# GpSimd issues the stores and loads of the attention's squares, and the first value projection goes by x tile in three column groups

## The chip, the core and the metric

The kernel runs on one core of one Trainium2 chip. The core has five engines with queues of their own, each executed in order: PE (TensorE, matrix products), DVE (VectorE), ACT (ScalarE), POOL (GpSimd) and SP (SyncE, which here only issues DMAs). DMAs are issued from SP's queue and from POOL's. The metric is the device time of one execution in microseconds (us); lower is better.

## The reference

A trunk of two layers works on 1024 tokens of width 1024. Layer 0 mixes tokens by chunked gated linear attention (GLA) with 4 heads, layer 1 by sparse attention with 16 heads in which an indexer lets each query see 256 keys. Both mixers are gated, projected back, added to the residual and normalized; a small gated term with a matrix `p` follows. Cut to what matters here:

```python
def gla_mixer(x, ...):                 # layer 0
    h = x @ w_in                       # q, k, v, z, a
    v = h[..., 2*qk : 2*qk + D_INNER]  # the value projection: 4 heads of 512 columns
    ...
def dsa_mixer(x, ...):                 # layer 1, blocks of 128 queries
    score = einsum(relu(qi @ ki), wi) ; idx = top_k(score, 256)
    logits = q @ k_sel * ATTN_SCALE    # 16 heads share one k and one v
    probs = softmax(logits)
    o = probs @ v_sel
    return (o * silu(z)) @ w_out

x = layer_norm(ALPHA * x + mixer(x))
x = x + (p[i] @ ple_w[i]) * sigmoid(x @ ple_gate_w[i])
```

All is float32. The kernel does each large product as three products of split parts: high times high, high times low, low times high.

## The kernel before

**Stages.** The sequence is cut into two halves of 512 tokens. Layer 0 runs half 0 and half 1, then layer 1 runs half 0 and half 1. In the times of the profile, layer 0's first half starts at 0, its second at about 525 us; layer 1's attention of the first half runs from about 1075 to 1390 us, of the second from about 1480 to 1860 us. "First half" and "second half" below mean these.

**Who sets the order.** The program is written by one planner (`Flow`): generators yield after each small group of PE products, and between groups a heap of due pieces is worked off. The due times are in the planner's own modelled time and decide only in which order instructions enter each engine's queue. On the chip each engine takes its queue in order and waits on semaphores.

**Layer 0's first block.** `v_phase` computes the values of one head: four PSUM banks (128 tokens each) are filled from eight tiles of x, which arrive in turn and are split into high and low parts. A weight pair (`whi`, `wlo`, taken by `W.take`) covers two x tiles: column group c of four holds x tiles 2c and 2c + 1 (kk = 0 and 1). Every step is three products (L58): xh times hi, xh times lo, xl times hi. The usual order is bank by bank with both x tiles in each; in group 0 of head 0, in either half, all four banks take x tile 0 first and then x tile 1.

**Layer 1's attention of one head.** `attend` makes the steps of one head. `A` computes the logits on PE and their minima on DVE (L1592), ACT takes the exponentials (L1599) into the tile `sq`, and DVE turns `sq` in blocks of 32 by 32 in place (L1605). The rest of the transposition goes through DRAM: `store` (L1618) writes each quarter of the partitions of `sq` to a DRAM tile `sqd`, four DMAs of 256 KB for each part, and `load` (L1628) reads that part back as `PT` in one DMA of 1 MB. The first half has one part per head, the second half two (`nb = half + 1`), so 4 stores and 1 load, or 8 stores and 2 loads. Then ACT copies each key group's high part to `ph` (L1645), DVE leaves the low part in `PT` (L1643), and PE multiplies both by the values (L58, `o<-ph,vT` and `o<-PT,vT`). There is one `sq`, `PT` has two buffers per part in the first half and one in the second. The logits of head h + 1 and its stores lie in the slot in which head h is multiplied by the values.

**The inverse sums.** For most heads DVE turns the row sums' inverses and POOL stores them to `row` in four tiny DMAs (L1664); for the others SP stores them (L1676). SP loads `row` to all partitions as `inv` (L1684), and DVE multiplies the gate by it (L1706).

**The queues.** SP issues the weights of layer 1 (L174, ready-made high and low parts from DRAM, 512 KB each, two tiles `whi` and `wlo` per block), the stores and loads of the squares, `inv` and the final stores. POOL issues, beside `row`: `xk` (L1279) and `ys` (L1260), which in layer 0's second half and the attention of the first half turn the residual for layer 1, and `y` (L1264), eight loads at the start of the attention of each half. POOL also clears `sq` (L1825) and does a few small operations of the norms. On each of the two queues the program uses eight semaphores in turn for its DMAs.

Of the kernel before, what the change touches and what calls it, by code (L numbers as in the profile page):

```python
# [10 lines left out]
F32 = mybir.dt.float32  # L11
# [36 lines left out]
class Flow:  # L48
# [6 lines left out]
    def mm(self, out, lhsT, rhs, start, stop):  # L55
        n = out.shape[-1] if len(out.shape) == 2 else math.prod(out.shape[1:])
        slow = lhsT.dtype != BF16 and (lhsT.dtype == F32 or n < 256)
        self.pe.matmul(out, lhsT, rhs, start=start, stop=stop)  # L58
        self.now += n * (4 if slow else 1) / 2400.0
# [218 lines left out]
def trunk_kernel(ctx, tc, x_tok, x_T, p_T, pos, freq, g_q, g_k, g_v, g_z, g_a, g_a2, g_ba, g_gn, g_o,  # L278
                 d_q, d_k, d_v, d_z, d_qi, d_ki, d_o, ln_gb, ple_c, gate_c, out):
    nc = tc.nc  # L280
    act, dve, pool = nc.scalar, nc.vector, nc.gpsimd
# [125 lines left out]
    def pbank():  # L407
        return psum[0].tile([128, 512], F32, tag="pb", name="pb", bufs=psum[1])
# [4 lines left out]
    def split(hi, lo, src, done=None):  # L413

        def second():
            lo_part(lo, src, hi)
            if done:
                done()
        chain((0, lambda: act.activation(hi, src, AF.Copy)), (0.9, second))  # L419
# [77 lines left out]
    def t2k(tag, dt=F32, bufs=8):  # L497
        return lp.tile([128, 512], dt, tag=tag, name=tag, bufs=bufs)
# [85 lines left out]
    def v_phase(u, X):  # L584
        h = u["h"]
        banks = [pbank(), pbank()] + [pp.tile([128, 512], F32, tag="U", name="U", bufs=2) for _ in range(2)]
        for c in range(4):
            hi, lo = W.take(("v", h, c))
            order = [(t, kk) for t in range(4) for kk in range(2)]
            if c == h == 0:  # L590
                order.sort(key=lambda x: x[1])
            for t, kk in order:
                ts = slice(t * 128, t * 128 + 128)
                xh, xl = X[2 * c + kk]
                ws = slice(kk * 512, kk * 512 + 512)
                first, last = c == 0 and kk == 0, c == 3 and kk == 1
                mm(banks[t], xh[:, ts], hi[:, ws], first, False)
                mm(banks[t], xh[:, ts], lo[:, ws], False, False)
                mm(banks[t], xl[:, ts], hi[:, ws], False, last)
                yield  # L600
                if last:
                    vh, vl = t2k("v", F32R), t2k("v", F32R)

                    def done(vh=vh, vl=vl, t=t):
                        u["v"][t] = vh, vl
                    split(vh, vl, banks[t], done)
# [731 lines left out]
    for half in range(NH):  # L1338
# [27 lines left out]
        for h, u in enumerate(units):  # L1366
# [4 lines left out]
            if h == 0:  # L1371
                fl.run(v_phase(u, X))
                for _ in feeder:
                    pass
                ready = a_phase(X, u.pop("wah"))
                if half == 0:
                    bg.set(rope_tables(), 1.7)

                def first_z():
                    zp = z_phase(u, X)  # L1380
                    for i, _ in enumerate(zp):
                        if i == 6:
                            fl.need(lambda: ready)
                            g_phase(u, ready[0])
                        yield
                fl.run(first_z(), qk_phase(u, X))
                g_load(1)
                load_y()
                if half == 0:
                    bg.finish()  # L1390
                    bg3.set(W.split_ahead(later, lp, xp), 2.06)
            else:
                fl.need(lambda: "w2" in u)
                g_phase(u, ready[0])
                fl.run(v_phase(u, X), qk_phase(u, X))
# [159 lines left out]
    def attend(st, h, half, ap, sq):  # L1555
# [11 lines left out]
        def get(*keys):  # L1567
            fl.req(*(k in st for k in keys))
            return [st[k] for k in keys]
# [40 lines left out]
        def store(i):  # L1610

            def f():
                get(*(("D", h, t) for t in range(4)))
                fl.req(st["x"] == nb * h + i)
                dt = st["dram", h, i] = dp.tile([4, 32, 4, HT], F32, tag=f"sq{i}", name="sqd", bufs=2)
                sq4 = sq.rearrange("p (b i c) -> p i b c", b=4, i=nb)
                for a in range(4):
                    nc.sync.dma_start(dt[:, :, a].rearrange("b p c -> p b c"), sq4[32 * a:32 * a + 32, i])  # L1618
                st["x"] += 1
            return f  # L1620

        def load(i):

            def f():
                dt, _ = get(("dram", h, i), ("dram", h, nb - 1))
                fl.req(st["pv"] >= (h * G - (0 if i else G - 4) if half else (h - 1) * G))
                PT = ap.tile([128, 4, HT], F32R, tag=f"PT{i}", name="PT", bufs=2 - half)
                nc.sync.dma_start(PT.bitcast(F32), dt.rearrange("b p a c -> (b p) a c"))  # L1628
                st["PT", h, i] = PT
            return f  # L1630

# [339 lines left out]
```

## Time and profile before

| what | value |
|---|---|
| median of three runs | 1935.55 us (1933.48 to 1938.89) |
| profiled execution: time, span | 1935.94 us, 1934.2 us |
| PE, PEld busy | 1914.7 us, 1590.6 us |
| DVE, ACT, POOL busy | 1495.4, 1002.4, 153.0 us |
| DMA issued by SP (q1), share of 16 engines | 474.55 MB, 72.1% |
| DMA issued by POOL (q0), share of 16 engines | 12.64 MB, 2.0% |

The span goes from the first to the last instruction; the rest of the profiled execution's time lies around it. In a row of a timeline the first number is the start in us from the span's start, the second the duration; a bracket at the end is the idle time of that engine just before and who ended it. In a row of DMA issues stand the number of DMAs, KB of each and the median time from issue to landing. In the view by stretches stand the stretch, its length, then busy time of PE, PEld (weight loads of PE), DVE, ACT and POOL with the number of instructions in brackets, the granted clock of PE, the share of the DMA engines that was busy and GB/s.

### The profile page before, as it was taken

How to read it: one execution, taken by the hardware profiler on the slowest of the kernel's cores; microseconds unless marked ns; L12 is line 12 of the kernel's file. 1: busy time of each engine (PE TensorE's matmuls, PEld its weight loads, DVE VectorE, ACT ScalarE, POOL GpSimd, SP SyncE). 2: the span in 40 equal slices, each digit the busy share in tenths (PEclk: the TensorE clock that was granted, in tenths of full speed). 3: DMA queues.
4: the chain of work that ended last, by engine and by line, in shares of the span. 5: the costliest groups of instructions: out<-in, count | busy, mean ns of one | idle time of the engine just before them, and what ended most of it. 6: DMA issues, size and time to landing. Idle time of an engine off the chain costs nothing.

```text
span 1934.2 us, 26875 instructions
## 1 busy us (share of the span) xinstructions
PE 1914.7 (99%) x8826; PEld 1590.6 (82%) x8826; DVE 1495.4 (77%) x3081; ACT 1002.4 (52%) x1896; POOL 153.0 (8%) x301
## 2 busy tenths in 40 slices
PE   9999999999999999999999999999999999999999
PEld 7888888888888888888888888888888778888887
DVE  5777666696778888878858987778798887777873
ACT  5564636445564646464535676756443443434432
POOL 0000000010010101010101001221001010000000
PEclk9999999999999999999999999999999999999999
DMA  4567766768667767677688588987877898888874
GB/s 156 207 218 230 225 220 215 225 207 274 223 221 262 244 224 247 222 242 228 211 287 302 169 294 288 318 293 283 305 247 283 324 305 302 299 303 289 290 285 142
DMA packets 200764, 488.91 MB, mean 253 GB/s; under 512 B 26504, under 2 KB 42928, under 8 KB 194480
## 3 DMA queue, kind: packets, MB, share of 16 engines
q1 hardware_dynamic: 193200, 474.55, 72.1%
q0 software_dynamic: 7424, 12.64, 2.0%
q8 instruction: 69, 1.13, 0.2%
q14 instruction: 71, 0.58, 0.1%
HBM read 343.18 MB, written 143.92 MB: 252 GB/s over the span
## 4 chain that ended last, share of the span: by engine, by line
PE 88%; DVE 5%; ACT 3%; DMA 2%; issue 1%; SPq 0%; DVEq 0%; ACTq 0%
PE pb L58 67%; PE o L58 8%; PE U L58 6%; PE S L58 5%; DMA PT<-sqd 1%; PE tr L58 1%; DVE sq L1605 1%; DVE PT L1643 0%; DMA wst<-in_g_v 0%; DVE sc L1141 0%; PE xt L62 0%; DVE wlo L191 0%; PE ix L58 0%; SPq L1618 0%; PE S L62 0%
## 5 line engine op out<-in xcount | busy, mean ns | idle before, releaser
L58 PE MATMUL pb<-x,whi 128*128 128x512 f32 x2272 | 704.2, 391 | 0.8 <-DVE x L411 0.7
L58 PEld LDWEIGHTS pb<-x,whi 128*128 128x128 f32 x2272 | 419.5, 188 | 80.0 <-DVE x L411 1.9
L58 PE MATMUL pb<-x,wlo 128*128 128x512 f32 x1136 | 442.6, 390 | 0.0
L58 PE MATMUL pb<-whi,u 128*128 128x512 f32 x1024 | 339.5, 392 | 1.5 <-ACT u L419 0.8
L58 PEld LDWEIGHTS pb<-x,wlo 128*128 128x128 f32 x1136 | 213.2, 188 | 45.8 <-DVE wlo L191 0.4
L58 PEld LDWEIGHTS pb<-whi,u 128*128 128x128 f32 x1024 | 192.2, 188 | 41.3 <-ACT u L419 1.2
L58 PE MATMUL pb<-wlo,u 128*128 128x512 f32 x512 | 199.6, 390 | 0.0
L191 DVE TENSOR_TENSOR wlo<-wst,whi 128x512 fp32r<-128x512 f32 x232 | 154.5, 683 | 35.1 <-ACT whi L189 34.9
L189 ACT ACTIVATE whi<-wst 128x512 fp32r<-128x512 f32 x232 | 136.4, 622 | 73.9 <-DMA wst<-in_g_k 28.8
L1599 ACT ACTIVATE sq<-P,mx 128x128 f32<-128x128 f32 (+7 forms) x128 | 98.8, 772 | 87.6 <-DVE mx L1592 58.0
L58 PE MATMUL S<-kT,q 128*128 128x512 f32 (+2 forms) x576 | 123.6, 343 | 1.7 <-DVE q L411 1.2
L1645 ACT ACTIVATE ph<-PT 128x512 fp32r<-128x512 f32 (+2 forms) x160 | 86.2, 558 | 63.0 <-PE o L58 43.4
L58 PEld LDWEIGHTS S<-kT,q 128*128 128x128 f32 x576 | 100.4, 188 | 20.5 <-DVE mx L1592 2.1
L58 PEld LDWEIGHTS pb<-wlo,u 128*128 128x128 f32 x512 | 96.2, 188 | 18.2
L1643 DVE TENSOR_TENSOR PT<-PT,ph 128x512 fp32r<-128x512 f32 (+2 forms) x160 | 92.6, 592 | 21.4 <-ACT ph L1645 21.2
L1207 ACT ACTIVATE tk<-sc,tki 128x768 f16<-128x768 f32 (+2 forms) x90 | 92.9, 1033 | 25.4 <-DVE tki L1216 21.6
L1605 DVE STREAM_TRANSPOSE sq<-sq 128x128 f32<-128x128 f32 (+7 forms) x128 | 97.7, 768 | 2.0 <-ACT sq L1599 2.0
L237 DVE TENSOR_TENSOR pst<-pst,phi 128x512 fp32r<-128x512 f32 x130 | 88.7, 682 | 7.4 <-ACT phi L233 7.4
L753 ACT ACTIVATE junk<-o 128x512 bf16<-128x512 f32 x32 | 19.1, 597 | 139.7 <-DVE ot L748 116.6
L58 PE MATMUL o<-ph,vT 128*128 128x512 f32 (+2 forms) x320 | 90.8, 365 | 0.0
L58 PE MATMUL pb<-whi,x 128*128 128x512 f32 x256 | 85.3, 392 | 0.0
L58 PE MATMUL U<-whi,x 128*128 128x512 f32 x256 | 84.6, 389 | 0.0
(330 smaller groups left out, 3400.4 us busy)
## 6 DMA issues: line engine op xcount, KB each, us to landing
whi<-whs SPq DMA_DIRECT2D x128, 512.0 KB, 6.1
wlo<-wls SPq DMA_DIRECT2D x128, 512.0 KB, 6.7
sqd<-sq SPq DMA_DIRECT2D x192, 256.0 KB, 4.4
PT<-sqd SPq DMA_DIRECT2D x48, 1024.0 KB, 7.7
whs<-phi SPq DMA_DIRECT2D x130, 256.0 KB, 4.1
wls<-pst SPq DMA_DIRECT2D x130, 256.0 KB, 4.1
wst<-in_g_z SPq DMA_DIRECT2D x32, 512.0 KB, 4.7
wst<-in_g_o SPq DMA_DIRECT2D x32, 512.0 KB, 5.1
```

The lines of the kernel that those rows point to most:

```text
L58: self.pe.matmul(out, lhsT, rhs, start=start, stop=stop)
L189: self.nc.scalar.activation(hi[:, c], st[:, c], AF.Copy, scale=1.0 if gain is None else gain)
L191: self.nc.vector.tensor_sub(lo[:, c], st[:, c], hi[:, c].bitcast(F32))
L237: self.nc.vector.tensor_sub(st, st.bitcast(F32), hi.bitcast(F32))
L753: act.activation(junk, ps, AF.Square, accum_out=u["ss"][:, c:c + 1])
L1207: act.activation(junk()[:, :n], scs[j], AF.Sign, bias=cand[:, j:j + 1].bitcast(F32), accum_out=cnt[:, j:j + 1])
L1599: act.activation(to, rows, AF.Exp, scale=-1.0, bias=mx, accum_out=sm[:, t:t + 1])
L1605: dve.transpose(x, x)
L1643: dve.tensor_sub(lo, lo.bitcast(F32), hi.bitcast(F32))
L1645: chain((0, lambda: act.activation(hi, lo.bitcast(F32), AF.Copy)), (0.8, second))
```

## The change

Two edits. In `v_phase` the condition of the order by x tile was group 0 of head 0 in either half; it is now groups 0, 1 and 2 of head 0 in the first half only. In `attend` the stores of the squares and their loads are issued by `pool` in place of `nc.sync`. Shapes, bytes, tiles and the due times of the planner are unchanged.

```diff
@@ v_phase
             order = [(t, kk) for t in range(4) for kk in range(2)]
-            if c == h == 0:
+            if c < 3 and h == u["half"] == 0:
                 order.sort(key=lambda x: x[1])
@@ attend, store
                 for a in range(4):
-                    nc.sync.dma_start(dt[:, :, a].rearrange("b p c -> p b c"), sq4[32 * a:32 * a + 32, i])
+                    pool.dma_start(dt[:, :, a].rearrange("b p c -> p b c"), sq4[32 * a:32 * a + 32, i])
@@ attend, load
                 PT = ap.tile([128, 4, HT], F32R, tag=f"PT{i}", name="PT", bufs=2 - half)
-                nc.sync.dma_start(PT.bitcast(F32), dt.rearrange("b p a c -> (b p) a c"))
+                pool.dma_start(PT.bitcast(F32), dt.rearrange("b p a c -> (b p) a c"))
```

On PE, group 1 of the first block. `pb_155`, `pb_156`, `U_157` and `U_158` are the four banks, `x_165` and `x_166` the high and low part of x tile 2, `x_190` and `x_191` those of x tile 3. Before:

```order
L58 MATMUL pb_155<-whi_162,x_165 128x512
L58 MATMUL pb_155<-wlo_163,x_165 128x512
L58 MATMUL pb_155<-whi_162,x_166 128x512
L58 MATMUL pb_155<-whi_162,x_190 128x512
L58 MATMUL pb_155<-wlo_163,x_190 128x512
L58 MATMUL pb_155<-whi_162,x_191 128x512
L58 MATMUL pb_156<-whi_162,x_165 128x512
```

And now:

```order
L58 MATMUL pb_155<-whi_162,x_165 128x512
L58 MATMUL pb_155<-wlo_163,x_165 128x512
L58 MATMUL pb_155<-whi_162,x_166 128x512
L58 MATMUL pb_156<-whi_162,x_165 128x512
L58 MATMUL pb_156<-wlo_163,x_165 128x512
L58 MATMUL pb_156<-whi_162,x_166 128x512
L58 MATMUL U_157<-whi_162,x_165 128x512
```

The first product with x tile 3, and with it the second half of the weights' columns, moves from the fourth place to the thirteenth.

On SP, heads 1 and 2 of the second half, before; `whi` and `wlo` are weights, `sqd` the squares in DRAM:

```order
L1618 DMA sqd<-sq 32x4x512 x8
L1628 DMA PT<-sqd 128x2048 x2
L1676 DMA row<-uf 4x128
L174 DMA whi<-whs 128x1024
L174 DMA wlo<-wls 128x1024
L1684 DMA inv<-row 128x512
L1618 DMA sqd<-sq 32x4x512 x8
L174 DMA whi<-whs 128x1024
L174 DMA wlo<-wls 128x1024
L1628 DMA PT<-sqd 128x2048
```

On POOL, the start of the second half and heads 0 to 2, now (before, the eight `y` stood together and behind them only the `row` stores):

```order
L1264 DMA y<-ys_12411 128x512
L1618 DMA sqd<-sq 32x4x512 x8
L1628 DMA PT<-sqd 128x2048
L1264 DMA y<-ys_12635 128x512
L1264 DMA y<-ys_12840 128x512
L1264 DMA y<-ys_13062 128x512
L1264 DMA y<-ys_13280 128x512
L1628 DMA PT<-sqd 128x2048
L1618 DMA sqd<-sq 32x4x512 x8
L1628 DMA PT<-sqd 128x2048 x2
L1618 DMA sqd<-sq 32x4x512 x8
L1664 DMA row<-sums 4x32 x4
```

The stores and loads of the squares left SP, where weights stood between the stores and the load. On POOL the four `row` stores stand between a head's stores and its loads, and in head 0 four of the eight `y` loads stand between its two loads.

## The prediction

> **What bounds the kernel now.** I began with the page's busy times by engine.
>
> ```profile
> PE 1914.7 (99%) x8826; PEld 1590.6 (82%) x8826; DVE 1495.4 (77%) x3081; ACT 1002.4 (52%) x1896; POOL 153.0 (8%) x301
> ```
>
> TensorE (PE) is busy for 99% of the span, POOL for 8%. So a change can give back only the time in which PE stands still. The view by stretches tells where that is: attention of layer 1's first half (1075 to 1390), the opening heads of its second half (1480 to 1600), the rest of that half. In the second column is the PE's busy time.
>
> ```profile
> 1075.00:1390.00 315.00, 311.83 (x1475) 261.71 (x1474) 253.79 (x654) 202.69 (x449) 39.89 (x75) 1.00 0.82 284
> 1480.00:1600.00 120.00, 115.93 (x538) 94.74 (x537) 97.84 (x207) 51.11 (x99) 7.95 (x16) 1.00 0.92 319
> 1600.00:1860.00 260.00, 259.98 (x1211) 217.32 (x1211) 200.91 (x416) 105.56 (x197) 17.85 (x36) 1.00 0.88 304
> ```
>
> PE is idle for 3.17, 4.07 and 0.02 us. The DMA share, last but one, is 0.82 to 0.92: the transfers leave little room. The waits of PE and the timelines of SP, ACT and PE around head 2 of the second half show one such idle stretch from its cause on; head 9 is the case without one.
>
> ```profile
> PE o L58 <- DVE PT L1643: 5.2, 6, 1.6
> 1522.57 7.42 SPq L1618 DMA_DIRECT2D sqd<-sq  x8
> 1530.10 0.69 SPq L174 DMA_DIRECT2D whi<-whs  x1
> 1530.90 1.18 SPq L174 DMA_DIRECT2D wlo<-wls  x1
> 1532.18 0.38 SPq L1628 DMA_DIRECT2D PT<-sqd  x1
> 1532.18 8.35 DMA PT<-sqd
> 1540.55 0.63 ACT L1645 ACTIVATE ph<-PT 128x512 fp32r<-128x512 f32 x1 [3.36 <-DMA PT<-sqd]
> 1544.16 0.50 PE L58 MATMUL o<-PT,vT 128*128 128x512 f32 x1 [0.53 <-DVE PT L1643]
> ...
> 1690.66 6.77 SPq L1618 DMA_DIRECT2D sqd<-sq  x8
> 1697.60 5.04 SPq L1628 DMA_DIRECT2D PT<-sqd  x2
> 1711.54 0.65 DVE L1643 TENSOR_TENSOR PT<-PT,ph 128x512 fp32r<-128x512 f32 x1
> 1715.26 0.39 PE L58 MATMUL o<-PT,vT 128*128 128x512 f32 x1
> ```
>
> In head 2 SP needs 7.42 us for eight stores, then issues two weight loads, and the first load of the squares goes out 1532.18 - 1522.57 = 9.61 us after the stores began. It lands 8.35 us on, ACT has waited 3.36 us for it, and PE waits behind DVE's low part. In head 9 no weights stand ahead: 1697.60 - 1690.66 = 6.94 us, and the low part is ready at 1712.19, 3.07 us before PE takes it. No row of PE's waits names a weight load.
>
> **The order by x tile.** Group 1 of the first block, as the trace has it:
>
> ```profile
> 13.23 0.62 PE L58 MATMUL pb<-whi,x 128*128 128x512 f32 x2
> 13.35 0.68 DVE L191 TENSOR_TENSOR wlo<-wst,whi 128x512 fp32r<-128x512 f32 x1
> 14.09 0.50 PE L58 MATMUL pb<-wlo,x 128*128 128x512 f32 x1 [0.24 <-DVE wlo L191]
> 527.61 0.68 DVE L411 TENSOR_TENSOR x<-y,x 128x512 fp32r<-128x512 f32 x1
> 532.33 0.73 PE L58 MATMUL ix<-v,u 128*128 128x512 f32 x2 [1.70 <-DVE v L411]
> ```
>
> The two products at 13.23 share 0.62 us; the second lasts some 0.39, as the single one at 1715.26 does, so they start 0.23 us apart and the next could start at 13.69. It starts at 14.09, when the low part of the weights' second half (ended 14.03) is there. By x tile, eleven more products on the first half stand between, 11 x 0.23 = 2.5 us: **-0.4 us**. Group 2 has no wait to lose. The condition also takes the order from group 0 of the second half: there the second x tile's low part (ready at 528.29) is wanted after three products instead of twelve, up to half a us early, but PE stops for 1.70 us at 532.33 anyway, for DVE: 0. If that cover is gone it costs 0.5.
>
> **Stores and loads on POOL.** 192 stores and 48 loads change the queue; bytes and form stay. The prices:
>
> ```profile
> sqd<-sq SPq DMA_DIRECT2D x192, 256.0 KB, 4.4
> od<-ot SPq DMA_DIRECT2D x116, 64.0 KB, 2.7
> ys<-xk POOLq DMA_DIRECT2D x64, 64.0 KB, 3.3
> xst<-x2s SPq DMA_DIRECT2D x8, 256.0 KB, 6.2
> xk<-x2s POOLq DMA_DIRECT2D x16, 256.0 KB, 6.2
> row<-sums POOLq DMA_DIRECT2D x88, 0.5 KB, 3.7
> L1260 POOL DMA_DIRECT2D ys<-xk x32 | 17.8, 563 | 126.5 <-DVE xk L1256 126.5
> 1467.04 3.85 POOL L1264 DMA_DIRECT2D y<-ys  x7
> 1475.45 0.54 POOL L1264 DMA_DIRECT2D y<-ys  x1 [4.56 <-DMA y<-ys]
> DMA to landing us min/median/max: 8.1/9.9/12.6
> ```
>
> POOL issues a store of the same form (32 partitions, four rows each) in 0.56 us; SP's eight took 0.93 each. For landing, the pair of 64 KB stores says +0.6 us on POOL, the pair of 256 KB loads 0. Seven `y` loads went out in a row on POOL and the eighth waited 4.56 us for the first to land: I take seven in flight as the limit. In that burst (the last row) loads landed after 8.1 to 12.6 us, which bounds the price from above: +1.9 or more over 6.2. I take +0.6 for a store, 5.0 in all, because that pair has its form, and 0 for a load.
>
> A head of the second half then runs so: seven stores by 3.9 us, the eighth when the first has landed, 5.0, issued by 5.6; the four `row` stores, behind them in POOL's order, 2.0; the first load at 7.6 (the stores it reads landed at 3 x 0.56 + 5.0 = 6.7). Against 9.61 in head 2 that is 2.0 us earlier; against 6.94 in head 9 it is 0.7 later, inside 3.07. So only 1480 to 1600 can gain. Its 4.07 us of idle PE are partly DVE's own, since DVE works 97.84 of 120; I take half: **-2.0 us**, between 0 and -4.07.
>
> What is behind the stores on POOL now? First `row`, for which `inv` on SP waits:
>
> ```profile
> 1524.45 2.02 POOL L1664 DMA_DIRECT2D row<-sums  x4 [48.45 <-DVE sums L1660]
> 1534.62 0.58 SPq L1684 DMA_DIRECT2D inv<-row  x1
> ```
>
> It would be issued from 1528.2 to 1530.2 and land 3.7 later, at 1533.9: still ahead of `inv`, cost 0. Second, in head 0 of the second half four `y` loads move behind the first load and ahead of the second. They take 4 x 0.55 = 2.2 us of issue and put 1 MB in front of a 1 MB load that SP issued here:
>
> ```profile
> 1480.99 7.29 SPq L1618 DMA_DIRECT2D sqd<-sq  x8
> 1492.82 0.62 SPq L1628 DMA_DIRECT2D PT<-sqd  x1
> ```
>
> POOL reaches it at 1481.0 + 6.7 + 0.6 + 2.2 = 1490.5, earlier than 1492.82 by 2.3; the 1 MB ahead costs, by the burst's spread ((12.6 - 8.1) / 6 + 0.54 = 1.29 us a load), 5.2. So it is 2.9 later, of which part shows: **+1.0 us**, between 0 and 2.9. Third, `xk` and `ys` of the first half wait behind squares; they serve a later stage, cost 0.
>
> First half: four stores, then the load.
>
> ```profile
> 1193.22 2.71 SPq L1618 DMA_DIRECT2D sqd<-sq  x4
> 1199.44 0.34 SPq L1628 DMA_DIRECT2D PT<-sqd  x1
> ```
>
> SP: 6.22 us from first store to load. POOL: 6.7, so 0.5 later in each of 16 heads. Most have cover in the PE's other products; heads without it pay: **+0.5 us**, between 0 and 16 x 0.5 = 8.
>
> On SP the weights no longer queue behind the squares. Since no PE wait is for weights, that is worth 0 by itself.
>
> The page "DMA: Bandwidth & Descriptors" of the Trainium skill, section "Issuing engines are not separate DMA queues", says that transfers started by any engine run on the same 16 DMA engines and interleave, and that several issuers save only issue time. The shares of 0.82 to 0.92 bear on that; it speaks against the change: by it the faster rival below could win no more than the issue time, 7.4 - 4.5 = 2.9 us a head. Its section "Latency and other measured facts" puts the first byte at about 1 us for the software path and about 0.6 for the hardware path; a store would cost 0.4 more by that, where the rows say 0.6.
>
> **Sum.** -0.4 - 2.0 + 1.0 + 0.5 = -0.9 us. The profiled execution took 1935.94 us (span 1934.2 and 1.7 around it), so 1935.0; the median of the runs shown is 1935.55 (1933.48 to 1938.89).
>
> **Rivals.**
>
> Faster: the squares arrive early enough in both halves that PE stops waiting. It has -0.4, 4.07 and 3.17 to win, -7.6: 1928.3. For it speaks head 2, where the load stood behind weights; against it that the DMA engines are nearly full and that PE's waits in the first half have other owners too (DVE is busy 254 of 315 us there).
>
> Slower: POOL's queue brings the squares late. Place: heads 0 to 4 of the second half, where PE has no spare. If eight stores land like the `y` burst, the first after 8.1 instead of 5.0 us (+3.1) and the load 1.9 later, the gain of 2.0 becomes a loss of 3.0 per head. Five heads pay 2 to 3 us: +10 to +15, about 1947. It decides from the point where the first load lands later than now in those heads; beyond 3 us more, the later heads pay too. The burst's landing times speak for it, the short rows of `ys` and `row` against.
>
> DVE holds POOL back while it writes descriptors. If each issue stretched to the longest seen, eight stores would take 6.2 us instead of 4.5 and rows and loads 1 more: 2.7 a head, in the first five heads and again at 1947 or above. Against it:
>
> ```profile
> L1279 POOL DMA_DIRECT2D xk<-x2s x16: 538/558/777, 535.1 to 1300.8; - x16
> ```
>
> With DVE at 77% the longest of sixteen is 0.78 us, the median 0.56. The Trainium skill's page "SBUF — State Buffer", section "SBUF: two separate sides", warns of this: POOL cannot write descriptors while DVE runs an operation in a two-port mode, and such a DMA took 3100 ns instead of 620. The row shows no stretch of that size.
>
> Nothing moves: PT was not what PE waited for, and weights issued earlier take the bandwidth that the squares gain. That is 1935.5, and inside the forecast.
>
> **Chances.** Forecast with its near neighbours, 1930 to 1941: 0.61. Faster rival 0.17. Slower rival 0.18, DVE holding POOL 0.04. A measurement of this kernel tells 0.3%, 5.8 us, from no change: under 1929.7 counts as faster (0.17), over 1941.4 as slower (0.22), between as the same (0.61). The range for 8 in 10 runs from 1929 to 1946: it cuts half of each rival.
>
> **What would show it.** Right: PE at 14.09 no longer waits; the rows of L1618 stand on POOL at about 0.56 us; in head 2 the first load goes out 7 to 8.5 us after the first store; PE's idle time in 1480 to 1600 falls to about 2 to 3 us and stays near 0 after 1600. Wrong: landings of `sqd` above 6 us or of `PT` above 9 on POOL, new PE waits for PT after 1600, a stretched issue on POOL, or PE waits that name a weight load.

## The result, and the profile after

The changed kernel takes 1952.84 us (median of four runs, 1951.05 to 1957.19); the kernel before takes 1936.84 beside it (1933.48 to 1938.89). The ratio is 1.009, 95% interval 1.0077 to 1.0103: slower by 16 us, where 1935.0 was forecast, in a range of 1929 to 1946. The profiled execution took 1952.27 us with a span of 1950.5.

First the lines of the page after: busy time by engine, SP's DMA queue (packets, MB, share of 16 engines), the DMA issues (KB of one, median us to landing).

```profile
PE 1922.3 (99%) x8826; PEld 1592.9 (82%) x8826; DVE 1496.3 (77%) x3081; ACT 1001.0 (51%) x1896; POOL 286.1 (15%) x541
...
q1 hardware_dynamic: 158640, 373.87, 56.7%
...
sqd<-sq POOLq DMA_DIRECT2D x192, 256.0 KB, 5.7
PT<-sqd POOLq DMA_DIRECT2D x48, 1024.0 KB, 8.0
```

About 100 MB went from SP's queue (474.55 MB before) to POOL's. The view of the stores' line says how POOL issues them (ns, least, median, most):

```profile
L1618 POOL DMA_DIRECT2D sqd<-sq x192: 550/552/597, 1077.4 to 1858.0; - x192
```

That is the 0.56 us of the forecast, and never much more. But a store now lands after 5.7 us where it was 4.4, and a load after 8.0 where it was 7.7. PE works 7.6 us longer on the same 8826 products. The view by stretches after, in the columns of the prediction:

```profile
1075.00:1390.00 315.00, 308.78 (x1445) 257.11 (x1444) 251.07 (x648) 200.00 (x445) 88.57 (x163) 0.99 0.83 287
1480.00:1600.00 120.00, 113.93 (x515) 92.06 (x514) 93.90 (x199) 51.55 (x100) 35.83 (x66) 0.99 0.92 315
1600.00:1860.00 260.00, 256.22 (x1188) 213.32 (x1186) 198.19 (x415) 101.77 (x191) 79.90 (x148) 0.99 0.85 296
```

PE is idle for 6.22, 6.07 and 3.78 us, where it was 3.17, 4.07 and 0.02. All three stretches lost, and in all three the clock stands at 0.99 where it was 1.00. The waits after (us in total, times, longest), then the two rows of before that answer to them:

```profile
ACT ph L1645 <- DMA PT<-sqd: 52.5, 22, 5.3
...
ACT sq L1599 <- DMA row<-sums: 33.4, 6, 10.3
...
ACT sq L1599 <- DMA sqd<-sq: 16.1, 5, 7.7
```

```profile
ACT sq L1599 <- DMA sqd<-sq: 19.0, 5, 7.1
...
ACT ph L1645 <- DMA PT<-sqd: 17.6, 8, 5.7
```

The squares are late at both ends. ACT waits 52.5 us for loaded squares (17.6 before). And it waits 49.5 us (33.4 + 16.1, before 19.0) before it may write the next head's exponentials, because the single tile `sq` is not free until its stores have landed.

**Where PE lost the time.** Matching the two traces product by product gives how much later each PE product starts than the same one before: -0.4 us at the end of layer 0, +5.8 behind the attention of the first half, +12.6 at 1610 us of before, +12.2 at 1800, +16.3 at the end. So layer 0 ends 0.4 ahead; the first half of the attention lost 6.2, heads 0 to 4 of the second half 6.8 (head 0 lost 4.5 and head 3 3.3, while around head 2 PE made up 1.2), heads 5 to 13 nothing, heads 14 and 15 another 4.1. The rows of PE at these places, and behind them the stretches that follow three of the stops:

```profile
1373.94 0.85 PE L58 MATMUL o<-ph,vT 128*128 128x512 f32 x2 [2.29 <-ACT ph L1645]
...
1512.81 0.50 PE L58 MATMUL o<-PT,vT 128*128 128x512 f32 x1 [2.02 <-DVE PT L1643]
...
1574.69 0.50 PE L58 MATMUL o<-PT,vT 128*128 128x512 f32 x1 [1.12 <-DVE PT L1643]
...
1850.37 0.73 PE L58 MATMUL o<-ph,vT 128*128 128x512 f32 x2 [1.26 <-ACT ph L1645]
```

```profile
1373.90:1377.40 3.50, 3.46 (x9) 2.55 (x10) 2.15 (x5) 3.50 (x7) 0.73 (x2) 0.57 1.00 403
1514.40:1517.30 2.90, 2.90 (x8) 2.24 (x7) 2.17 (x6) 2.35 (x5) 1.10 (x2) 0.50 0.99 307
1852.70:1855.40 2.70, 2.70 (x6) 2.14 (x7) 2.70 (x4) 1.43 (x3) 1.24 (x3) 0.50 0.92 360
```

Behind three of these stops, of 2.29, 2.02 and 1.26 us, the granted clock (third from the end) is about half for some 3 us. If the time lost is the share of the clock that was not granted, these three bouts cost 3.50 x 0.43 + 2.90 x 0.50 + 2.70 x 0.50 = 4.3 us, a quarter of the loss, and they count as busy PE.

**One head from its cause on.** Head 3 of the second half after, on SP, POOL and ACT:

```profile
1557.47 0.32 SPq L174 DMA_DIRECT2D whi<-whs  x1
...
1554.94 4.47 POOL L1618 DMA_DIRECT2D sqd<-sq  x8 [9.02 <-DVE z L1528]
...
1564.43 0.56 POOL L1628 DMA_DIRECT2D PT<-sqd  x1 [1.45 <-PE S L58]
1568.93 0.54 POOL L1628 DMA_DIRECT2D PT<-sqd  x1 [3.94 <-DMA sqd<-sq]
...
1568.61 0.83 ACT L1599 ACTIVATE sq<-P,mx 128x640 f32<-128x640 f32 x1 [10.30 <-DMA row<-sums]
```

And the same head before:

```profile
1545.33 7.48 SPq L1618 DMA_DIRECT2D sqd<-sq  x8
1553.12 3.29 SPq L1628 DMA_DIRECT2D PT<-sqd  x2
1556.45 0.43 SPq L174 DMA_DIRECT2D whi<-whs  x1
...
1556.33 0.83 ACT L1599 ACTIVATE sq<-P,mx 128x640 f32<-128x640 f32 x1 [7.10 <-DMA sqd<-sq]
```

Before, the weights stood on SP behind the loads, and a load waits until its stores have landed: the weights of this head went out at 1556.45, when all eight stores were done. After, nothing on SP waits for the squares. The weights go out at 1557.47, in the midst of the stores. The stores are issued sooner (4.47 us instead of 7.48) and land later, the slowest 9.5 us after its issue instead of 4.9: the second load, which waits for the last of them, goes out 1568.93 - 1554.94 = 14.0 us after the first store, against at most 1556.41 - 1545.33 = 11.1 before. ACT writes the next head's first exponentials 13.7 us after the first store instead of 11.0. (ACT's wait is put down to `row`, the latest event by the profile; POOL's row at 1568.93 names the stores.) Which queue used the transfer engines meanwhile says the view of the queues from the first store on, after (1554 to 1566; the last stores land some 2 us later still) and before (1545 to 1556, when the last store lands):

```profile
q0 software_dynamic: 605, 1.99, 61.9%
q1 hardware_dynamic: 308, 1.13, 24.4%
```

```profile
q1 hardware_dynamic: 1435, 3.15, 93.3%
```

After, 1.13 MB of SP's traffic went beside the squares. Before, one queue carried nearly everything, and the weights of this head came behind the squares in it.

The stop in the first half (1373.94) shows the same, on SP, POOL and ACT:

```profile
1357.04 0.33 SPq L174 DMA_DIRECT2D whi<-whs  x1
...
1356.42 2.22 POOL L1618 DMA_DIRECT2D sqd<-sq  x4 [10.84 <-DVE sq L1605]
...
1367.37 0.55 POOL L1628 DMA_DIRECT2D PT<-sqd  x1 [6.71 <-PE pb L58]
...
1366.66 0.40 ACT L1599 ACTIVATE sq<-P,mx 128x128 f32<-128x128 f32 x1 [4.43 <-DMA sqd<-sq]
```

Four weight loads, 2 MB, go out from 1357.04 to 1362.10, beside the four stores. ACT's row says that the stores landed about 10 us after the first was issued. The load goes out 1367.37 - 1356.42 = 10.95 us after the first store; before, in the same head, it was 1359.38 - 1353.22 = 6.16, with these weights behind it. (POOL's row names PE as the last to end its wait; the load could in any case not go out before the stores had landed.)

### The profile page after: what moved, and what is told of

Its sections match the earlier page's. It is cut to its first block, busy times and chain, and to the rows that moved or that the text cites. A ratio compares the mean times of both kernels' runs of the same rounds, so it can differ in the third digit from the quotient of the medians.

```text
span 1950.5 us, 26933 instructions
## 1 busy us (share of the span) xinstructions
PE 1922.3 (99%) x8826; PEld 1592.9 (82%) x8826; DVE 1496.3 (77%) x3081; ACT 1001.0 (51%) x1896; POOL 286.1 (15%) x541
## 3 DMA queue, kind: packets, MB, share of 16 engines
q8 instruction: 69, 1.13, 0.2%
## 4 chain that ended last, share of the span: by engine, by line
PE 83%; DVE 7%; DMA 6%; ACT 2%; issue 2%; POOL 0%; SPq 0%; DVEq 0%; ACTq 0%; POOLq 0%
PE pb L58 63%; PE o L58 7%; PE U L58 6%; PE S L58 4%; DMA PT<-sqd 4%; DVE sq L1605 1%; DMA sqd<-sq 1%; PE tr L58 1%; DVE PT L1643 1%; DVE sc L1141 1%; DVE wlo L191 0%; DMA wst<-in_g_v 0%; DVE P L1592 0%; PE xt L62 0%; PE S L62 0%
## 5 line engine op out<-in xcount | busy, mean ns | idle before, releaser
L1618 POOL DMA_DIRECT2D sqd<-sq x192 | 106.0, 557 | 341.1 <-DVE sq L1605 212.4
L1645 ACT ACTIVATE ph<-PT 128x512 fp32r<-128x512 f32 (+2 forms) x160 | 86.1, 559 | 94.8 <-DMA PT<-sqd 52.5
L1207 ACT ACTIVATE tk<-sc,tki 128x768 f16<-128x768 f32 (+2 forms) x90 | 92.8, 1032 | 21.6 <-DVE tki L1216 17.8
L796 POOL TENSOR_SCALAR rs<-ss 128x1 f32<-128x1 f32 x32 | 8.8, 274 | 631.6 <-ACT junk L753 631.6
```

Source lines behind the costliest of these rows:

```text
L1207: act.activation(junk()[:, :n], scs[j], AF.Sign, bias=cand[:, j:j + 1].bitcast(F32), accum_out=cnt[:, j:j + 1])
L1618: pool.dma_start(dt[:, :, a].rearrange("b p c -> p b c"), sq4[32 * a:32 * a + 32, i])
L1645: chain((0, lambda: act.activation(hi, lo.bitcast(F32), AF.Copy)), (0.8, second))
```

## The experiments

Two theories were set against each other. **Sharing:** SP's load, by waiting for the stores, also held the weights back; without it the weights share the transfer engines ("the wires" below) with the squares. (This wait of SP is called the hold below.) **Latency:** POOL's queue brings each transfer late by itself. All times below are medians beside runs of the kernel before on the same chip, whose medians were 1935.8 to 1936.3 us. "Later by" is again the start of PE's products against the trace of before.

### The parts of the change

The order by x tile alone (`if c < 3 and h == u["half"] == 0:` in `v_phase`):

> The order by x tile alone; squares and their loads stay on SP. Theory of the queue (POOL brings the squares late, and all of the loss comes from there): 0.4 to 0.8 us faster than before, about 1935, because PE's starts were 0.79 us ahead at 94 us in the changed kernel and 0.36 ahead after the second half of layer 0. Rival (the new order in the first block shifts the work against the transfers, and that makes the attention lose time): slower by several us. Nothing of the loss here leaves all 16 us to the queue.

1935.46 us, ratio 0.9996 (0.9986 to 1.0005): no measurable effect. The order is not the cause of the loss.

The queue alone (`pool.dma_start` for stores and loads):

> Stores and loads of the squares on POOL alone; the order of the first block as before. Theory of the queue: slower by 16 to 17 us, about 1953, with PE idle about 6 us in layer 1's first half of attention and about 6 us in heads 0 to 4 of the second, and a granted clock of about 0.5 for some 3 us behind each stop of about 2 us. Rival (both edits are needed): clearly less than 16 us.

1953.58 us, ratio 1.0089 (1.0074 to 1.0105): all of the loss, 17.8 us.

The stores alone on POOL:

> Only the stores of the squares on POOL; their loads on SP, behind weights again. Theory of the store's latency (a store on POOL lands later, 5.7 us by the median where it was 4.4, and the load waits for it): most of the loss is here, 8 to 16 us, 1944 to 1952, and the first load goes out as late after the first store as in the changed kernel. Moreover a load on SP that waits for a store now holds the weights behind it on SP. Rival (the loads are what is late, because they stand behind the y and row transfers of POOL): within 3 us of before.

1942.84 us, ratio 1.0031 (1.0019 to 1.0042): 7.0 us. The loss lies wholly in the first half of the attention: 8.4 later behind it, 6.2 at 1610. Heads 0 to 4 of the second half won 2.2 us. Neither expectation had this. SP's load kept its hold here, so in the first half the hold alone does not make POOL's stores free; at one of the two stops there, 2.90 us at 1382.66, PE waits for `z`, and DVE had waited 5.52 us for `inv`, which comes up again below.

The loads alone on POOL:

> Only the loads of the squares on POOL; the stores on SP. Theory of the store's latency: small, 0 to 5 us slower, since the first load can go out at the time of before or earlier (no weights ahead on SP), and only head 0 of the second half pays for the y loads that now stand ahead of its second load (about 3 to 4 us with the slow clock behind the stop). Rival (the loads are what is late): most of the 16 us, about 1950.

1948.89 us, ratio 1.0054 (1.0037 to 1.0071): 13.1 us, the larger part. The expectation from the store's latency missed; but that loads on POOL are late for standing behind `y` and `row` does not follow yet, since with the load SP's wait went too.

By stage:

```diff
-                    nc.sync.dma_start(dt[:, :, a]...          # the stores
+                    (pool if half else nc.sync).dma_start(dt[:, :, a]...
-                nc.sync.dma_start(PT...                       # the loads
+                (pool if half else nc.sync).dma_start(PT...
```

> Stores and loads of the squares on POOL in the second half alone (two stages of eight stores and two loads a head), on SP in the first half. From the drift of PE's starts in the changed kernel the second half's share is about 10 of 16 us (5.8 us were lost by 1407 us, 6.6 from there to 1582, 4.2 at 1842 and after): about 1946. If the loss of the second half only follows from the first half's late end (the rival), it is near 1937.

1944.81 us, ratio 1.0045 (1.003 to 1.006): 8.6 us, about half. The second half's loss does not hang on the first half's.

### Giving SP its wait back

In place of the load that left SP, SP copies 64 numbers of the stored squares to a spare DRAM tile. The copy moves 256 bytes, but it waits for the four stores as the load did:

```diff
+                seen = dp.tile([4, 16], F32, tag="seen", name="seen", bufs=2)
+                nc.sync.dma_start(seen, dt[0, 0, :, 0:16])
                 pool.dma_start(PT.bitcast(F32), dt.rearrange("b p a c -> (b p) a c"))
```

Stores and loads on POOL in both halves, with the copy:

> Stores and loads of the squares on POOL as in the kernel with the queue alone (1953.6 us), but where SP issued the load before, SP now issues a copy of 64 numbers out of the squares just stored. It has to wait until the four stores have landed, and so it holds back the weights behind it on SP, as the load on SP did. Theory of sharing (what makes the squares late is that weights, now free of the load's wait, run beside the stores and share the wires with them): most of the 17.7 us comes back, 1937 to 1943; stores land in about 4 to 5 us again. Theory of latency (POOL's queue is slow by itself, or its rows and y loads are in the way): nothing comes back, about 1953.

1945.5 us, ratio 1.0048 (1.0033 to 1.0063): 8 of the 17.8 us came back. From 1440 to 1800 us this kernel lost 0.8 us (7.4 to 8.2 later); without the copy, in the trace of the queue alone, it lost 6.1 (10.9 to 17.0).

Stores on SP, loads on POOL, with the copy:

> Stores on SP, loads on POOL (1948.9 us without more), and where SP issued the load before, SP now issues the copy of 64 numbers out of the squares, which holds the weights behind it back until the stores have landed. Theory of sharing: that hold is most of what SP's load did for the time; 1937 to 1941, losses in heads 0 to 4 and 14 and 15 of the second half go. Theory that a load on POOL is slow by itself (it landed after 8 to 9.6 us there, and after 7.7 to 8.7 us on SP in the same heads): nothing comes back, about 1949.

1944.47 us (1941.06 to 1949.52), ratio 1.0043 (1.0029 to 1.0057): 5 of 13.1 us came back, fewer than the theory of sharing had it. What the other 8 us are was not separated, and the runs spread over 8.5 us.

Stores and loads on POOL in the second half alone, with the copy:

> Stores and loads on POOL in the second half alone (1944.8 us without more), and there SP issues the copy of 64 numbers out of the squares where it issued the load, which holds the weights back until the stores have landed. Theory of sharing: most of the 8.6 us comes back, 1936 to 1939, and the stops at 1565 to 1571 (3.1 us together) and at 1842 to 1845 (2.3 us) go. Theory that a load on POOL lands late by itself: nothing comes back, 1943 to 1946.

1938.35 us, ratio 1.0013 (1.0004 to 1.0023): 6 of the 8.6 us came back by this one wait. Head 3 of the second half, on SP and POOL, without the copy and then with it; behind each the least, median and greatest time from issue to landing of its eight stores:

```profile
1550.17 0.32 SPq L174 DMA_DIRECT2D whi<-whs  x1
...
1547.64 4.49 POOL L1618 DMA_DIRECT2D sqd<-sq  x8 [8.58 <-DVE z L1528]
...
1561.60 0.54 POOL L1628 DMA_DIRECT2D PT<-sqd  x1 [2.39 <-DMA sqd<-sq]
...
DMA to landing us min/median/max: 3.0/6.8/9.5
```

```profile
1554.49 4.50 SPq L1630 DMA_DIRECT2D seen<-sqd  x2
1559.09 0.38 SPq L174 DMA_DIRECT2D whi<-whs  x1
...
1547.87 4.49 POOL L1618 DMA_DIRECT2D sqd<-sq  x8 [9.50 <-DVE z L1528]
...
1558.89 0.54 POOL L1631 DMA_DIRECT2D PT<-sqd  x1 [1.15 <-PE S L58]
...
DMA to landing us min/median/max: 3.0/5.5/6.5
```

With the copy the weights go out at 1559.09 instead of beside the stores, the second load 1558.89 - 1547.87 = 11.0 us after the first store instead of 14.0, and it no longer waits for the stores. The slowest store lands after 6.5 us instead of 9.5. The stops of PE at 1565 to 1571 fell to one of 0.76 us, and those at 1842 to 1845 are gone. In the second half, sharing is shown as the main cause. What the copy left, about 2.6 us, is mostly head 0 (0.5 later at 1500 us, 4.3 at 1512).

### What else is in the loss

`y` on SP (`nc.sync.dma_start(y[:, k], ...)`), with all squares on POOL:

> As the kernel with the queue alone, but the y loads of the second halves go out on SP, so that no y load stands ahead of the second load of head 0 on POOL. Theory that POOL's order costs something there: head 0 of the second half no longer waits 4.6 us for its second load, 3 to 4 us come back with the slow clock behind the stop, about 1950. Rival (the y loads take the same wires whoever issues them): no change, 1953.

1956.36 us, ratio 1.0107 (1.0091 to 1.0124): nothing came back. The same stop stands in head 0 of the second half:

```profile
1515.23 0.80 PE L58 MATMUL o<-PT,vT 128*128 128x512 f32 x1 [2.00 <-DVE PT L1643]
```

So the place of `y` on POOL's queue is not what that head pays for. (On SP the `y` loads still use the same wires; that was not taken away.)

In the first half, stores and loads on POOL with the copy (1945.5 us) still lost 6.9 us (0.5 to 7.4 later), though the hold worked there too. In the head of the stop at 1373.94 the load went out 1362.58 - 1355.17 = 7.4 us after the first store, where it was 1371.88 - 1360.56 = 11.3 with the queue alone, and PE no longer stops for it (2.44 us with the queue alone). The trace of the kernel with the copy names another transfer in its place. PE, the row of DVE for which it waited, and two rows of SP:

```profile
1381.67 0.50 PE L58 MATMUL pb<-whi,u 128*128 128x512 f32 x1 [4.00 <-DVE z L1528]
...
1378.46 0.69 DVE L1708 TENSOR_TENSOR z<-z,inv 128x512 f32<-128x512 f32 x1 [5.83 <-DMA inv<-row]
...
1363.39 0.38 SPq L174 DMA_DIRECT2D whi<-whs  x1
...
1365.71 0.32 SPq L1686 DMA_DIRECT2D inv<-row  x1
```

SP lets the held weights go in a burst from 1363.39 on; `inv` stands behind four of them and is issued at 1365.71, but lands only 12.7 us later, at 1378.46. The next head's stores run on POOL meanwhile. So `inv` was moved to POOL (`pool.dma_start(st["inv", h], ...)`):

> The kernel with stores and loads on POOL and the copy on SP (1945.5 us), with the broadcast of the sums' inverses (inv) on POOL too, behind the four row stores that it reads, and no longer behind the weights on SP. In that kernel PE's longest stop, 4.00 us at 1381.67, waited for z, and z had waited 5.8 us for inv. Theory that inv stands behind the burst of weights that SP lets go after its hold: the stop goes, and with the slow clock behind it 4 to 6 us, 1939.5 to 1941.5. Rival (inv lands late because its row does, or shares the wires with the next head's stores on POOL): the stop stays, 1945; and the loads behind inv on POOL may come later still.

1941.89 us, ratio 1.0027 (1.0016 to 1.0037): 3.6 us came back, slightly less than expected; the stop at 1381 is gone, and DVE's row of `z` shows how:

```profile
1372.71 0.69 DVE L1708 TENSOR_TENSOR z<-z,inv 128x512 f32<-128x512 f32 x1 [0.38 <-DMA inv<-row]
```

I read this as the same collision, with `inv` as its victim. It is not shown by itself: the run moves `inv` ahead of the weights and onto another queue at once. The 5.6 us that this kernel still loses were not separated: a load on POOL that shares with SP's burst, POOL's own latency and head 0 of the second half are left, and no run here tells them apart.

### Stores on POOL, loads on SP

If SP keeps the load, it keeps the hold. First, all stores of the second half on POOL:

> Only the stores of the second half on POOL; its loads, and both in the first half, on SP. With the stores alone on POOL in both halves PE was busy 117.58 of 120 us in 1480 to 1600 (115.93 before), and the losses lay in heads 3 to 5 and 15 of the first half. Theory of sharing (SP's load still waits for the stores and holds the weights back): 0 to 2 us faster than before, 1934 to 1936, since eight stores are issued in 4.5 us instead of 7.4 and nothing else runs beside them. Theory of latency: the stores land 1 to 2 us later in each head, and heads 0 to 4 lose 3 to 6 us: 1939 to 1942.

1936.42 us, ratio 1.0003 (0.9993 to 1.0012): no difference. 128 stores on POOL's queue cost nothing that can be measured, so in the second half latency of POOL's stores is not the cause either. (In the first half stores alone on POOL did cost, as above.) But nothing was won: by product the trace gains 3.8 us in heads 1 to 4, and loses 2.6 in head 0 and 2.0 in the last two heads. PE stood for 2.02 us at 1505.69 in head 0, where four `y` loads were issued on POOL behind the stores and ran beside the first load. Whether they are the reason was not tried.

Then two of four stores on POOL and two on SP, in the second half, together with the order by x tile:

```diff
                 for a in range(4):
-                    nc.sync.dma_start(dt[:, :, a]...
+                    (pool if half and a % 2 else nc.sync).dma_start(dt[:, :, a]...
```

> The order by x tile, and in the second half two of every four stores on POOL and two on SP; all loads on SP, so that SP still holds the weights back until all stores have landed. Eight stores are then issued in about 3.7 us instead of 7.4. If the issue time of the stores delays the squares of heads 0 to 4: 1 to 3 us faster, 1932.5 to 1934.5. If the transfers set the landing (the theory of sharing: 1 MB at some 200 GB/s takes 5 us whoever issues it): no more than the order's 0.4, about 1935.5.

1932.05 us, ratio 0.9975 (0.9965 to 0.9985): **faster than before by 4.2 us**, more than expected. Head 2 of the second half, whose first load the prediction had followed, on SP, POOL and ACT, and behind it the stretch of heads 0 to 4:

```profile
1524.02 2.48 SPq L1618 DMA_DIRECT2D sqd<-sq  x4
...
1531.14 1.19 SPq L1628 DMA_DIRECT2D PT<-sqd  x1
...
1524.40 2.21 POOL L1618 DMA_DIRECT2D sqd<-sq  x4 [19.32 <-DVE sq L1605]
...
1539.63 0.63 ACT L1645 ACTIVATE ph<-PT 128x512 fp32r<-128x512 f32 x1 [0.22 <-DMA PT<-sqd]
```

```profile
1480.00:1600.00 120.00, 117.89 (x547) 97.93 (x546) 99.14 (x212) 52.78 (x101) 23.68 (x44) 0.99 0.91 323
```

The eight stores are out after 2.6 us instead of 7.42, the first load 7.1 us after the first store instead of 9.61, and ACT waits 0.22 us for it instead of 3.36. PE is idle for 2.11 us in the stretch, where it was 4.07. Whether the sooner issue does this, or that two queues carry the squares, was not separated.

The split alone, without the order:

> Two of every four stores of the second half on POOL and two on SP, loads on SP, the order of the first block as before. If the gain of 4.2 us seen with the order by x tile comes from the stores' issue time: 3 to 4.5 us faster than before, about 1932.5. If it came from the order and the way the two meet: within 1.5 us of before.

1932.49 us, ratio 0.9983 (0.9974 to 0.9992): 3.3 us faster. The gain is the split's; what the order adds to it is too small to tell.

The order and the split in both halves (`pool if a % 2 else nc.sync`):

> The order by x tile and the split of two and two in both halves. If POOL issues part of the stores at no cost as long as SP's load still holds the weights: 1931 to 1932.5, since four stores of the first half are issued in 1.9 us instead of 2.7 to 3.7, but PE has little to win there. If POOL's stores in the first half get in the way of inv and of the weights, as in the kernel with all stores on POOL (stops of 2.8 us at 1178 and 2.9 us at 1383): slower by 3 to 7 us than with the split in the second half alone, 1935 to 1939.

1932.24 us, ratio 0.9981 (0.9973 to 0.999): 3.6 us faster. The first half neither gains nor loses by it.

## Why the prediction was wrong, point by point

- **What bounds the kernel.** Right: PE is busy, gains can only come from the idle 7 us of the attention, and heads 0 to 4 of the second half have no spare. Heads 5 to 13 lost nothing, as their spare of 3 us had it. But head 9 was taken for all the later heads, and heads 14 and 15 lost 4.1.
- **The order by x tile, -0.4.** The mechanism was right: the wait at 14.09 is gone, and PE's row of that place after has no bracket (below). The size can't be told. PE ends layer 0 0.4 us ahead, but in the trace of the split alone, which leaves the order as it was, it ends 1.1 ahead; alone the edit gave 0.9996.

```profile
14.04 0.39 PE L58 MATMUL pb<-whi,x 128*128 128x512 f32 x1
```

- **Stores and loads on POOL, 4.4 to 5.0 us and +0.** The issue time was right. In head 2, which the forecast had followed, the first load went out 1541.62 - 1532.86 = 8.76 us after the first store: sooner than the 9.61 of before, but not the 7.6 forecast. In head 3 it was 1564.43 - 1554.94 = 9.5. Mis-sized was the landing: 5.7 by the median, and 9.5 for the slowest store of head 3. The prices came from transfers of other stages, and the stores' 4.4 us on SP had been measured where SP's load held the weights back.
- **"On SP the weights no longer queue behind the squares. Since no PE wait is for weights, that is worth 0 by itself."** This is the step that failed. The prediction saw the weights leave their place behind the squares and asked only whether PE waits for weights. What weights that go earlier collide with got no term in the sum; the last rival let them take bandwidth from the squares, but only as much as the squares would gain, for no change. In the second half the collision was worth about 6 us: 1944.81 without the hold, 1938.35 with it. In the first half the hold took away PE's stop for the squares, but `inv` then came late, and 6.9 us stayed lost; how much of the changed kernel's 6.2 us there is the collision stays open. The page "DMA: Bandwidth & Descriptors" of the Trainium skill, section "Queues, rings and completion order", says that each DMA engine goes round between the queues that have work for it. That both queues moved data in the same 12 us of head 3, 1.99 and 1.13 MB, agrees with it. The prediction had cited another section of that page for the same engines being shared, and used it as a ceiling on the gain; it was the price.
- **`row` before the load, cost 0; `y` ahead of the second load, +1.0.** `y` on POOL was indeed not what cost: `y` on SP gave nothing back. But the +1.0 was mis-sized: head 0 lost 4.5 us, with half the clock behind its stop. No run moved `row`; in head 3 its four stores took from 1559.89 to 1562.98, 3.1 us instead of 2.0, ahead of the load. And `inv` landed late in the first half where the stores were on POOL and SP held the weights; moving it gave 3.6 us back. In the changed kernel itself PE's stop in the first half (1373.94) was for the load.
- **First half, +0.5, between 0 and 8.** Mis-sized: 6.2 us in the changed kernel. That this lies inside the bounds is luck: they were 0.5 us in each of 16 heads, and 4.3 of the 6.2 came with the one stop at 1373.94 and the slow clock behind it.
- **The limit of seven in flight** did not bind in head 3, where eight stores went out in 4.47 us. In head 0 POOL stood for 2.94 us before the eighth store, and in head 1 for 0.40 and 0.30 us before the last two; only the last of these rows names a store's landing. What the forecast left out is that the `row` stores wait, too:

```profile
POOL row L1664 <- DMA sqd<-sq: 9.9, 14, 1.4
```

A `row` store reads nothing of the squares. But the program uses eight semaphores in turn on POOL, so the eighth DMA behind a store waits until that store has landed, and the load stands behind the `row` stores.
- **-2.0 in heads 0 to 4.** The split bears the mechanism out, with -3.3 us in all: when the eight stores go out sooner, the squares come sooner. It needed the loads to stay on SP. In the changed kernel itself PE made up 1.2 us around head 2, and lost more in heads 0 and 3.
- **The slower rival** named the direction, the place (heads 0 to 4) and a time of 1947, but put it down to POOL's own queue. In the second half POOL's stores by themselves cost nothing (1.0003); the 7 us that the stores alone cost (1.0031) lie in the first half, and what part of that is POOL's own was not separated. The rival also left out heads 14 and 15 and the slow clock. DVE holding POOL back is ruled out by the stores' issue times, 597 ns at most.

## What to carry to other kernels

A wait in an in-order queue can be useful: a load that waits for its stores also keeps less urgent transfers off the wires. Before moving a DMA to another queue, list what stood behind its wait, ask when that will go out now and which urgent transfer will then be in flight, not only whether anyone waits for it. To save issue time, split the issues over two queues and leave the waiting one where it was.

## What the runs showed of the hardware that was not expected

The clock: in these traces every bout of half the clock lasted 3.4 us, and the length of the stop ahead of it did not decide whether it came. In the changed kernel a stop of 2.29 us at 1373.94 had one behind it (0.57, above). At the same place of the program, in the kernel with the queue alone, a stop of 2.44 us had none:

```profile
1378.49 0.73 PE L58 MATMUL o<-ph,vT 128*128 128x512 f32 x2 [2.44 <-ACT ph L1645]
...
1378.50:1384.00 5.50, 5.50 (x27) 4.34 (x28) 4.11 (x12) 4.77 (x11) 0.64 (x2) 1.00 0.90 367
```

And the kernel with the split and the order, which is faster than before, has such a bout 1.9 us behind a stop of only 1.53 us at 1504.76 (0.50 from 1506.70 to 1510.10). What decides was not found; a bout cost here some 1.5 us beyond the stop. The Trainium skill's page "TensorE: Matmul & The Clock Gate", section "HAM oscillation — how this bites in real kernels", puts the limit at idle gaps of some 3.4 us; here stops well below that had a bout behind them.

The median time from issue to landing also misled: it hardly moved for the loads (7.7 to 8.0 us), while what had to land ahead of them decided when they were issued at all.
